# Attention layers: the queries' norm factor moved into the scale of the row extremes, and the keys' second copy made by a transfer

## The chip, the cores and the metric

The kernel runs on one core of a Trainium2 chip. The metric is device time in microseconds. The kernel before was timed three times: 1247.73, 1248.68 and 1249.45 us, median 1248.68.

## The reference

A decoder trunk of four pre-norm residual layers over 256 tokens of width 1024, all in float32. Each layer adds a token mixer and then a SwiGLU feed-forward part. The mixers are, in order: native sparse attention (layer 0), block attention (layer 1), a short gated convolution (layer 2), and native sparse attention again (layer 3). What matters here is that every part begins with a norm, and that the attention scores are a softmax over scaled products of queries and keys:

```
def rms_norm(x, g):
    y = xf * lax.rsqrt(jnp.mean(xf * xf, axis=-1, keepdims=True) + RMS_EPS)
    return (y * g.astype(jnp.float32)).astype(x.dtype)
...
a = rms_norm(h, norm_mix[i])
q, k_c, v_c, k_s, v_s, k_w, v_w, gates = jnp.split(a @ w_in, NSA_SPLITS, axis=-1)
q = q.reshape(B_, S_, G, R, dh) * (HEAD_DIM ** -0.5)
s_win = jnp.einsum('bnqgrd,bnkgd->bgrnqk', qb, kwb)
p_win = masked_softmax(s_win, wmask)
```

The sparse attention has 16 query heads in 4 key groups of 64 elements. It adds three results per head with gates: attention over compressed keys (15 blocks made by a small two-layer network), over selected blocks, and over a window. With 256 tokens the last two see the same causal mask and differ in their keys and values. The block attention is a causal attention with 16 heads here.

## The kernel before, in words

The activations are kept transposed (channels on the 128 partitions, 256 tokens along the free dimension), in eight pieces. The norm is split. Its gain is multiplied in before the projections (`prep`). Its per-token factor, `rstd`, is only known later, so it is multiplied into each projection's result: `rms_tokens` (L239) makes `rstd` with tokens on partitions, `rms_rows` (L246) spreads it as `rb`, the same 256 factors on every partition, and `scaled` (L409) multiplies a projection's result in PSUM with `rb` into an SBUF row. That multiplication is L411.

Precision is kept by splitting each float32 operand into a rounded high part and a remainder, the low part. A weight part of 8 tiles of 128x128 is loaded (`load_part`, L98), its high part copied by ScalarE (L119) and its low part subtracted by VectorE or GpSimd (L123). A product then takes three matmuls (`mm3`, L143 to L145): high with high, high weight with low activation, low weight with high activation. `take` (L126) hands out weight tiles in stream order; it also runs the jobs that are queued in `self.jobs` once the stream has come to the part that they name.

In the sparse attention (`nsa`, L549) the order of steps is written out by hand in `NSA_ORDER`: K is a projection of keys, q one of queries (two heads each, eight in all), F, E, C and D the compression network, c the attention over compressed keys, V the values, s the scores of two heads with their softmax, t and T transposes, P the product with the values. The Tile framework then schedules: it keeps to this order as a priority but puts on each engine's queue what it reckons ready first. The queues, SyncE's DMA queue among them, run strictly in that planned order.

The scores in the sparse attention are taken with one matmul of full depth for the high parts: a query tile holds the high part of one head on 64 partitions and its low part on the other 64 (`project_q`, L612 to L620). For that the keys must stand on both halves of the partitions. `put_keys` (L581 to L590) scales a key projection, and for each of its two groups writes the high part to its own half (L587) and to the other half (L588) with ScalarE, and the low part to both halves with two VectorE subtractions (L590). There are four key projections in each sparse layer, so 8 groups.

`scores` (L761) fills three PSUM banks with tag A, of which there are four; a projection takes one of the same four. `softmax` (L432) then works on each head in four pieces: for each piece one VectorE instruction adds the mask, multiplies by -0.125 and takes the row minimum (L441), ScalarE takes the exponential with its sum (L444), VectorE the reciprocal (L446), and GpSimd multiplies by the reciprocal and the gate (L448). That makes 64 L441 instructions in a sparse layer and 32 in the block layer, where `moba` (L474) has its own `project_q` (L494) that splits a scaled query. `compressed` (L702) adds a mask to the compressed scores with tokens on partitions (L717).

Of the kernel before, what the change touches and what calls it, by code (L numbers as in the profile page):

```python
# [9 lines left out]
F32 = mybir.dt.float32  # L10
F32R = mybir.dt.float32r
AF = mybir.ActivationFunctionType
OP = mybir.AluOpType
# [3 lines left out]
P = 128  # L17
D = 1024
S = 256
KT = D // P  # L20
NT = S // P
# [4 lines left out]
QSCALE = 0.125  # L26
NEG = -3.0e38
PART = 8
# [20 lines left out]
LAG = 4  # L49
PROJ_BANKS = "AABB"  # L50
PR = ["gpsimd"]
KEY_LO = ["vector", "vector"]
OWN = "vava"
CONE = "vector"
NPAIR = 8
# [4 lines left out]
class Kernel:  # L60
# [178 lines left out]
    def rms_tokens(self):  # L239
        nc = self.nc  # L240
        v = self.sb([P, NT], "var")
        nc.vector.tensor_scalar(v, self.sums[:, :NT], 1.0 / D, EPS, op0=OP.mult, op1=OP.add)
        self.rstd = self.sb([P, NT], "rstd")
        nc.gpsimd.tensor_tensor(out=self.rstd, in0=v, in1=self.mhalf, op=OP.pow)

    def rms_rows(self):  # L246
        nc = self.nc
        pb = self.bank("B")
        for t in range(NT):
            nc.tensor.transpose(pb[:, t * P:(t + 1) * P], self.rstd[:, t:t + 1].to_broadcast([P, P]), self.ident)  # L250
        self.rb = self.sb([P, S], "rb", bufs=1)
        nc.vector.tensor_copy(self.rb, pb[:, :S])
# [179 lines left out]
    def softmax(self, cols, gates):  # L432

        nc = self.nc
        pr = self.sb([P, 3 * S], "pr", bufs=PR_BUFS)
        mn = self.sb([P, 4], "mn", bufs=3)
        den = self.sb([P, 4], "den", bufs=3)
        rc = self.sb([P, 4], "rc", bufs=3)
        for j, (src, c) in enumerate(cols):
            n = c.stop - c.start  # L440
            nc.vector.tensor_tensor_reduce(pr[:, c], src, self.mask[:, S - n:], -QSCALE, 3.0e38, OP.add, OP.min,  # L441
                                           mn[:, j:j + 1])
        for j, (src, c) in enumerate(cols):
            nc.scalar.activation(pr[:, c], pr[:, c], AF.Exp, bias=mn[:, j:j + 1],  # L444
                                 scale=-1.0, accum_out=den[:, j:j + 1])
        nc.vector.reciprocal(rc, den)  # L446
        for j, (src, c) in enumerate(cols):
            getattr(nc, PR[j % len(PR)]).tensor_scalar(pr[:, c], pr[:, c], rc[:, j:j + 1], gates[j], op0=OP.mult, op1=OP.mult)  # L448
        return pr
# [24 lines left out]
    def moba(self, norm):  # L474
        nc, at = self.nc, self.begin(norm)
# [17 lines left out]

        def project_q(p):  # L494
            q = self.ff([P, 2, S])
            self.project([lambda x: self.split(q, self.scaled(x))], at)
            qs.append(q)

        def scores(p):
# [28 lines left out]
        def weigh(p):  # L528
# [8 lines left out]
            for i in range(2):  # L537
# [4 lines left out]
            outs.append(d)  # L542

        self.steps(MOBA_ORDER, {"V": lambda _: self.values(at, put_values), "k": project_k, "q": project_q,
                                "s": scores, "T": turn, "P": weigh})
        self.out_proj(outs, norm + 1)


    def nsa(self, j, norm):  # L549
        nc, at = self.nc, self.begin(norm)  # L550
# [9 lines left out]
        for a in range(2):  # L560
            nc.gpsimd.memset(xs[a][:, 512:], 0.0)
            x = xs[a][:, 512:640].rearrange("p (r c) -> p r c", c=16)
# [15 lines left out]
            self.project([put_raw(a, gp) for a in range(2) for gp in range(2)], at)  # L578


        def put_keys(b, gp):  # L581
            def put(p):
                f = self.scaled(p)
                for i in range(2):
                    kk = self.keys[2 * gp + i]
                    r, o = slice(i * DH, (i + 1) * DH), slice((1 - i) * DH, (2 - i) * DH)
                    nc.scalar.copy(kk[r, 0, b, :], f[r])  # L587
                    nc.scalar.copy(kk[o, 0, b, :], f[r])  # L588
                    for eng, d in zip((getattr(nc, e) for e in KEY_LO), (r, o)):
                        eng.tensor_tensor(out=kk[d, 1, b, :], in0=f[r], in1=kk[r, 0, b, :].bitcast(F32),  # L590
                                          op=OP.subtract)
            return put

        gates = self.sb([P, NT, 48], "gates", bufs=1)
# [17 lines left out]
        def project_q(_):  # L612
            q = self.ff([P, 2, S])

            def put(p):
                f = self.scaled(p)
                for i in range(2):
                    r, o = slice(i * DH, (i + 1) * DH), slice((1 - i) * DH, (2 - i) * DH)
                    nc.scalar.copy(q[r, i, :], f[r])
                    nc.vector.tensor_tensor(out=q[o, i, :], in0=f[r], in1=q[r, i, :].bitcast(F32), op=OP.subtract)  # L620

            self.project([put], at)
            qs.append(q)
# [3 lines left out]
        pc = []  # L627
# [74 lines left out]
        def compressed(gp):  # L702

            p = self.bank(CMP_BANK)
            for i in range(8):
                q = qs[4 * gp + i // 2][:, i % 2, :]
                for n, c in enumerate((112, 240)):
                    mm(p[:, :S], zk[:, 2 * gp + i // 4, c - 16 * i:c - 16 * i + P], q, start=(i == 0 and n == 0),
                       stop=(i == 7 and n == 1))
            sc = self.row()  # L710
            nc.scalar.copy(sc, p[:, :S])
            pq = self.bank(CMP_BANK)
            for t in range(NT):
                nc.tensor.transpose(pq[:, t * P:(t + 1) * P], sc[:, t * P:(t + 1) * P], self.ident)
            pc = self.row()
            p3 = pc.rearrange("p (h c) -> p h c", c=16)
            nc.vector.tensor_tensor(out=pc, in0=pq[:, :S], in1=self.cneg, op=OP.add)  # L717
            mx = self.sb([P, 16], "cmx")
            bc = mx[:, :, None].to_broadcast([P, 16, 16])
            nc.vector.tensor_reduce(out=mx, in_=p3, op=OP.max, axis=AX.X)  # L720
            nc.vector.tensor_tensor(out=p3, in0=p3, in1=bc, op=OP.subtract)
            nc.scalar.activation(pc, pc, AF.Exp, scale=QSCALE)
            getattr(nc, CONE).tensor_tensor(out=pc, in0=pc, in1=self.cone, op=OP.mult)
            nc.vector.tensor_reduce(out=mx, in_=p3, op=OP.add, axis=AX.X)
            nc.vector.tensor_scalar(mx, mx, 1e-30, None, op0=OP.max)
            nc.vector.reciprocal(mx, mx)
            m2 = mx.rearrange("p (t h) -> p t h", t=NT)
            nc.vector.tensor_tensor(out=m2, in0=m2, in1=gates[:, :, 8 * gp:8 * gp + 8], op=OP.mult)
            nc.vector.tensor_tensor(out=p3, in0=p3, in1=bc, op=OP.mult)
            ph = self.sb([P, 16, 2, 16], "ph", F32R, bufs=1)  # L730
            nc.scalar.copy(ph[:, :, 0, :], p3)
            nc.vector.tensor_tensor(out=ph[:, :, 1, :], in0=p3, in1=ph[:, :, 0, :].bitcast(F32), op=OP.subtract)
            phs.append(ph)
# [88 lines left out]
        def project_keys(i):  # L822
            self.project([put_keys(i // 2, i % 2)], at)
# [220 lines left out]
```

## Time and profile before

| | |
|---|---|
| timed runs | 1247.73, 1248.68, 1249.45 us |
| span of the profiled execution | 1247.6 us |
| busy: TensorE, VectorE, ScalarE, GpSimd | 1225.3, 875.0, 675.6, 227.3 us |
| weight loads | 384 of 512 KB, 4.3 us each to landing |
| mean DMA rate | 182 GB/s |

No separate time is given for the profiled execution beside its span; the median of the timed runs is 1.1 us above that span. In the groups of instructions a row names the line, the engine and operation, what it writes and reads, the shape and the count; then the busy time in us and the mean duration in ns, and after the last bar the idle time of the engine just before and what ended it. In a timeline row the first number is the start in us from the span's start, the second the duration. A matmul's duration there includes the depth of the pipeline: matmuls start every 0.12 us for 256 columns and every 0.23 us for 512, though one is listed with 0.28 or 0.39. So a busy TensorE may still be standing, and its stalls are read from the waits and the starts. `PEclk` is the granted TensorE clock, 1.00 at full speed.

### The profile page before, as it was taken

How to read it: one execution, taken by the hardware profiler on the slowest of the kernel's cores; microseconds unless marked ns; L12 is line 12 of the kernel's file. 1: busy time of each engine (PE TensorE's matmuls, PEld its weight loads, DVE VectorE, ACT ScalarE, POOL GpSimd, SP SyncE). 2: the span in 40 equal slices, each digit the busy share in tenths (PEclk: the TensorE clock that was granted, in tenths of full speed). 3: DMA queues.
4: the chain of work that ended last, by engine and by line, in shares of the span. 5: the costliest groups of instructions: out<-in, count | busy, mean ns of one | idle time of the engine just before them, and what ended most of it. 6: DMA issues, size and time to landing. Idle time of an engine off the chain costs nothing.

```text
span 1247.6 us, 19344 instructions
## 1 busy us (share of the span) xinstructions
PE 1225.3 (98%) x6788; PEld 1061.5 (85%) x6788; DVE 875.0 (70%) x1653; ACT 675.6 (54%) x1218; POOL 227.3 (18%) x357
## 2 busy tenths in 40 slices
PE   8999999999999999999999999999999999999997
PEld 8987888888899888888888888888899878888886
DVE  7778785665778795656769886565747797756553
ACT  5588754544456544545444545454446896555443
POOL 1067600000111520000113210000220676000000
PEclk9998999999999999999999999999999999999999
DMA  8741166767555347666665666776666312676772
GB/s 288 247 126 49 52 220 198 239 198 231 188 170 153 102 140 209 216 212 208 220 196 167 195 201 195 212 236 195 208 204 210 118 38 71 208 228 213 226 224 72
DMA packets 91585, 227.20 MB, mean 182 GB/s; under 512 B 17504, under 2 KB 38368, under 8 KB 91488
## 3 DMA queue, kind: packets, MB, share of 16 engines
q1 hardware_dynamic: 91056, 225.41, 57.6%
q8 instruction: 53, 0.87, 0.3%
q10 hardware_dynamic: 432, 0.56, 0.1%
q14 instruction: 44, 0.36, 0.1%
HBM read 213.33 MB, written 1.05 MB: 172 GB/s over the span
## 4 chain that ended last, share of the span: by engine, by line
PE 87%; DVE 5%; ACT 4%; POOL 2%; issue 1%; DMA 1%; POOLq 0%; ACTq 0%; DVEq 0%
PE psA L163 13%; PE psA L167 7%; PE psB L347 6%; PE psB L349 6%; PE psB L348 6%; PE psA L348 5%; PE psA L349 5%; PE psA L347 5%; PE psA L143 2%; PE psB L640 2%; PE psA L144 2%; PE psA L145 2%; PE psB L163 2%; DVE wlo L123 2%; PE psC L349 2%; PE psC L347 2%
## 5 line engine op out<-in xcount | busy, mean ns | idle before, releaser
L123 DVE TENSOR_TENSOR wlo<-raw,whi 128x1024 fp32r<-128x1024 f32 (+1 forms) x366 | 441.0, 1215 | 261.7 <-ACT whi L119 213.7
L119 ACT CAST whi<-raw 128x1024 fp32r<-128x1024 f32 (+1 forms) x379 | 393.2, 1039 | 425.9 <-PE psC L349 91.3
L163 PE MATMUL psA<-ff,whi 128*128 128x512 f32 x686 | 181.5, 393 | 0.1
L163 PEld LDWEIGHTS psA<-ff,whi 128*128 128x128 f32 x686 | 124.6, 189 | 22.7 <-DVE row L847 0.6
L347 PE MATMUL psB<-whi,at 128*128 128x512 f32 x352 | 137.6, 391 | 0.2 <-ACT pr L304 0.2
L349 PE MATMUL psB<-whi,at 128*128 128x512 f32 x352 | 137.2, 390 | 0.0
L348 PE MATMUL psB<-wlo,at 128*128 128x512 f32 x352 | 137.1, 389 | 0.0
L230 POOL TENSOR_TENSOR ssq<-ssq,row 128x256 f32<-128x256 f32 x42 | 33.6, 799 | 393.0 <-ACT row L228 392.2
L143 PE MATMUL psA<-at,whi 128*128 128x256 f32 x352 | 101.3, 288 | 2.0 <-DVE row L411 2.0
L167 PE MATMUL psA<-ff,wlo 128*128 128x256 f32 x686 | 101.5, 283 | 0.0
L167 PEld LDWEIGHTS psA<-ff,wlo 128*128 128x128 f32 x686 | 96.2, 191 | 5.3
L145 PE MATMUL psA<-at,wlo 128*128 128x256 f32 x352 | 99.9, 284 | 0.0
L144 PE MATMUL psA<-at,whi 128*128 128x256 f32 x352 | 99.9, 284 | 0.0
L349 PE MATMUL psA<-whi,at 128*128 128x512 f32 x256 | 99.7, 389 | 0.0
L347 PE MATMUL psA<-whi,at 128*128 128x512 f32 x256 | 99.7, 389 | 0.0
L348 PE MATMUL psA<-wlo,at 128*128 128x512 f32 x256 | 99.7, 389 | 0.0
L448 POOL TENSOR_SCALAR pr<-pr,rc,gates 128x256 f32<-128x256 f32 (+1 forms) x128 | 73.7, 590 | 112.6 <-DVE rc L446 111.3
L347 PEld LDWEIGHTS psB<-whi,at 128*128 128x128 f32 x352 | 66.1, 188 | 14.0 <-ACT pr L304 0.6
L349 PEld LDWEIGHTS psB<-whi,at 128*128 128x128 f32 x352 | 66.1, 188 | 13.8
L348 PEld LDWEIGHTS psB<-wlo,at 128*128 128x128 f32 x352 | 66.1, 188 | 13.6
L123 POOL TENSOR_TENSOR wlo<-raw,whi 128x256 fp32r<-128x256 f32 x96 | 69.6, 763 | 36.7 <-ACT whi L119 16.6
L444 ACT ACTIVATE pr<-pr,mn 128x128 f32<-128x128 f32 (+1 forms) x160 | 71.2, 448 | 5.7 <-DVE mn L441 5.0
(239 smaller groups left out, 2256.1 us busy)
## 6 DMA issues: line engine op xcount, KB each, us to landing
raw<-in_w SPq DMA_DIRECT2D x384, 512.0 KB, 4.3
pt<-pt SPq DMA_DIRECT2D x320, 32.0 KB, 3.1
wf<-in_w SPq DMA_DIRECT2D x16, 512.0 KB, 4.5
h<-in_xt SPq DMA_DIRECT2D x4, 256.0 KB, 4.5
raw<-in_w SPq DMA_DIRECT2D x4, 256.0 KB, 4.8
pt<-pt SPq DMA_DIRECT2D x64, 16.0 KB, 2.9
w<-in_w SPq DMA_DIRECT2D x2, 256.0 KB, 3.9
pt<-in_gfin SPq DMA_DIRECT2D x1, 512.0 KB, 3.9
```

Of the source, the lines that this page charges most:

```text
L119: copy(hi[:, c], src[:, c])
L123: eng.tensor_tensor(out=lo[:, d], in0=src[:, d], in1=hi[:, d].bitcast(F32), op=OP.subtract)
L143: mm(out, wt[0], act[0], start=first, stop=False)
L144: mm(out, wt[0], act[1], start=False, stop=False)
L145: mm(out, wt[1], act[0], start=False, stop=last)
L163: mm(outs[o], w[0], acts[k].rearrange("p i s -> p (i s)"), start=(k == 0), stop=(k == n - 1))
L167: mm(outs[o][:, :S], w[1], acts[k][:, 0, :], start=False, stop=False)
L347: mm(o, a[:, 0, s], hi, start=(k == 0), stop=False)
L348: mm(o, a[:, 0, s], lo, start=False, stop=False)
L349: mm(o, a[:, 1, s], hi, start=False, stop=(k == KT - 1))
L444: nc.scalar.activation(pr[:, c], pr[:, c], AF.Exp, bias=mn[:, j:j + 1], scale=-1.0, accum_out=den[:, j:j + 1])
L448: getattr(nc, PR[j % len(PR)]).tensor_scalar(pr[:, c], pr[:, c], rc[:, j:j + 1], gates[j], op0=OP.mult, op1=OP.mult)
```

## The change

It has these parts. The queries are no longer multiplied by the norm factor: `project_q` of both attentions splits the projection straight from PSUM. In its place `rms_tokens` makes a second column, `rneg`, which is `rstd` times -0.125, in the three attention layers' norms, and L441 uses it as its scale instead of the constant (tokens stand on the partitions there, so the factor of a row is one number per partition). In `compressed` the one addition of the mask becomes two of half the width that first multiply by `rstd`. The keys' copy on the other 64 partitions is no longer computed: each group's high and low part, 64 partitions with two runs of 1 KB, are copied by a DMA on SyncE's queue, which is queued as a job for the next weight part. Last, the framework's scratch for DMA descriptors is set to 1024.

```
@@ rms_tokens
+        if self.norm in (0, 2, 6):
+            self.rneg = self.sb([P, NT], "rneg")
+            nc.gpsimd.tensor_scalar(self.rneg, self.rstd, -QSCALE, 1.0, op0=OP.mult, op1=OP.mult)
@@ softmax
-            nc.vector.tensor_tensor_reduce(pr[:, c], src, self.mask[:, S - n:], -QSCALE, 3.0e38, OP.add, OP.min,
-                                           mn[:, j:j + 1])
+            nc.vector.tensor_tensor_reduce(pr[:, c], src, self.mask[:, S - n:], self.rneg[:, j // NT:j // NT + 1],
+                                           3.0e38, OP.add, OP.min, mn[:, j:j + 1])
@@ moba, project_q
-            self.project([lambda x: self.split(q, self.scaled(x))], at)
+            self.project([lambda x: self.split(q, x)], at)
@@ nsa
+        copies = []
+
+        def double():
+            while copies:
+                nc.sync.dma_start(*copies.pop(0))
+
         def put_keys(b, gp):
...
                     nc.scalar.copy(kk[r, 0, b, :], f[r])
-                    nc.scalar.copy(kk[o, 0, b, :], f[r])
-                    for eng, d in zip((getattr(nc, e) for e in KEY_LO), (r, o)):
-                        eng.tensor_tensor(out=kk[d, 1, b, :], in0=f[r], in1=kk[r, 0, b, :].bitcast(F32),
-                                          op=OP.subtract)
+                    nc.vector.tensor_tensor(out=kk[r, 1, b, :], in0=f[r], in1=kk[r, 0, b, :].bitcast(F32),
+                                            op=OP.subtract)
+                    copies.append((kk.bitcast(F32)[o, :, b, :], kk.bitcast(F32)[r, :, b, :]))
+                self.jobs.append((self.pos // PART + 1, double))
@@ nsa, project_q
-            def put(p):
-                f = self.scaled(p)
+            def put(f):
@@ compressed
-            nc.vector.tensor_tensor(out=pc, in0=pq[:, :S], in1=self.cneg, op=OP.add)
+            for t in range(NT):
+                c = slice(t * P, (t + 1) * P)
+                nc.vector.scalar_tensor_tensor(pc[:, c], pq[:, c], self.rstd[:, t:t + 1], self.cneg[:, c], op0=OP.mult,
+                                               op1=OP.add)
@@ kernel
-    nc = bacc.Bacc("TRN2", target_bir_lowering=False, num_devices=1)
+    nc = bacc.Bacc("TRN2", target_bir_lowering=False, num_devices=1, dynamic_dma_scratch_size=1024)
```

More of the change, by code (lines that the diff above doesn't have):

```diff
@@ L51 @@
 PR = ["gpsimd"]
-KEY_LO = ["vector", "vector"]
 OWN = "vava"
```

## The prediction

> **What bounds the kernel now.** I read the page first: span, busy time by engine, chain.
>
> ```profile
> span 1247.6 us, 19344 instructions
> PE 1225.3 (98%) x6788; PEld 1061.5 (85%) x6788; DVE 875.0 (70%) x1653; ACT 675.6 (54%) x1218; POOL 227.3 (18%) x357
> PE 87%; DVE 5%; ACT 4%; POOL 2%; issue 1%; DMA 1%; POOLq 0%; ACTq 0%; DVEq 0%
> ```
>
> TensorE carries 87% of the chain, and the change takes no matmul away. It can only win where TensorE stands, so I listed what TensorE waits for, and then cut the span into windows: the stretch from the end of the compression matmuls to the first scores in both sparse-attention layers (46 to 66, 949 to 969), the tails of both (100 to 123, 1015 to 1026), and the block-attention layer's tail.
>
> ```profile
> PE psB L786 <- POOL pr L448: 2.1, 4, 0.8
> PE psA L143 <- DVE row L411: 2.0, 2, 1.4
> core 0: us, PE busy (x) PEld busy (x) DVE busy (x) ACT busy (x) POOL busy (x), PEclk, DMA share, GB/s
> 46.00:66.00 20.00, 19.37 (x157) 18.66 (x156) 19.56 (x47) 13.92 (x29) 0.00 (x0) 1.00 0.57 187
> 100.00:116.00 16.00, 13.71 (x93) 11.21 (x91) 14.20 (x63) 15.35 (x54) 13.21 (x24) 0.99 0.21 67
> 116.00:123.00 7.00, 6.99 (x25) 5.50 (x26) 4.84 (x15) 3.81 (x13) 5.95 (x11) 0.54 0.00 1
> 949.00:969.00 20.00, 18.59 (x151) 17.88 (x150) 18.32 (x44) 13.73 (x27) 0.00 (x0) 1.00 0.58 180
> 1015.00:1026.00 11.00, 8.98 (x52) 6.44 (x51) 10.44 (x45) 10.31 (x36) 8.53 (x16) 1.00 0.16 48
> 418.00:440.00 22.00, 20.50 (x128) 17.28 (x127) 17.52 (x52) 12.11 (x40) 9.98 (x19) 1.00 0.28 88
> ```
>
> Two kinds of stall come out. In the key stretches VectorE is the full engine (19.56 of 20 us, 18.32 of 20), and the named wait is L411, the multiplication by the norm factor, with 2.0 us in two places. In the tails VectorE, ScalarE and GpSimd are all busy (10.44, 10.31 and 8.53 of 11 us), and TensorE stands for GpSimd's normalising multiply, L448, which the change does not touch. The two places of the L411 wait, from TensorE's timeline, with VectorE's work ahead of the longer one:
>
> ```profile
> 62.59 0.38 PE L143 MATMUL psA<-at,whi 128*128 128x256 f32 x1 [0.63 <-DVE row L411]
> 963.17 0.64 PE L767 MATMUL psA<-keys,ff 128*128 128x256 f32 x4
> 963.64 1.08 PE L770 MATMUL psA<-keys,ff 128*128 128x512 f32 x4
> 966.13 0.38 PE L143 MATMUL psA<-at,whi 128*128 128x256 f32 x1 [1.41 <-DVE row L411]
> ...
> 958.24 1.67 DVE L590 TENSOR_TENSOR keys<-row,keys 64x256 fp32r<-64x256 f32 x4
> 963.91 1.71 DVE L590 TENSOR_TENSOR keys<-row,keys 64x256 fp32r<-64x256 f32 x4
> 965.64 0.43 DVE L411 TENSOR_TENSOR row<-psA,rb 128x256 f32<-128x256 f32 x1
> ```
>
> At 963.17 a query projection is finished and the first scores begin; they take three of the four A banks. The next projection needs the fourth, which the query projection still holds: VectorE is busy with the keys (963.91) and reads that bank only at 965.64.
>
> **The change part by part.** The rows for the prices, by line and shape, and the shortest transfer inside SBUF:
>
> ```profile
> L590 DVE TENSOR_TENSOR keys<-row,keys 64x256 fp32r<-64x256 f32 x32 | 13.3, 417 | 1.1 <-ACT keys L587 0.5
> L588 ACT CAST keys<-row 64x256 fp32r<-64x256 f32 x16 | 6.5, 404 | 0.4
> L411 DVE TENSOR_TENSOR row<-psA,rb 128x256 f32<-128x256 f32 x46 | 19.0, 420 | 3.5 <-PE psA L145 2.9
> L441 DVE CUSTOM_DVE_ANT_0 pr<-psA,mask 128x256 f32<-128x256 f32 x80 | 31.7, 416 | 0.3 <-PE psA L508 0.2
> L859 DVE TENSOR_SCALAR row<-gu,cw 128x256 f32<-128x256 f32 x8 | 2.8, 354 | 0.3
> L652 DVE TENSOR_SCALAR row<-row 128x256 f32<-128x256 f32 x2 | 0.6, 288 | 0.0
> L620 DVE TENSOR_TENSOR ff<-row,ff 64x256 fp32r<-64x256 f32 x32 | 13.7, 427 | 1.8 <-ACT ff L619 0.9
> L541 DVE TENSOR_TENSOR ff<-psC,ff 64x256 fp32r<-64x256 f32 x16 | 6.7, 418 | 3.6 <-ACT ff L540 3.2
> L540 ACT CAST ff<-psC 64x256 fp32r<-64x256 f32 x16 | 5.9, 367 | 10.1 <-PE psC L145 7.5 <-DVE ff L541 2.5
> L244 POOL TENSOR_TENSOR rstd<-var,mhalf 128x2 f32<-128x2 f32 x8 | 6.6, 822 | 106.3 <-DVE var L242 106.3
> pt<-pt SPq DMA_DIRECT2D x320, 32.0 KB, 3.1
> ```
>
> *Keys.* Half of the 32 subtractions L590 and all 16 copies L588 go: per sparse layer 8 x 0.417 = 3.3 us of VectorE and 8 x 0.404 = 3.2 us of ScalarE. All of it lies before the values' projection; two of the four key projections (2 x 2 x 0.417 = 1.7 us of VectorE) lie between 958 and 966.
>
> *Queries.* 24 multiplications L411 go (8 in each sparse layer, 8 in the block layer): 0.42 us each, 0.34 where nothing depends on the one before (below). What read the SBUF row now reads PSUM: by L541 beside L620 a subtraction costs the same (418 and 427 ns), by L540 beside L588 a copy 0.04 us less. [...]
>
> *Row extremes.* 160 L441 instructions take their scale from a column instead of a constant. No row shows that form. The nearest are one operation with a column and with a constant: L859 354 ns, L652 288, so 66 ns more. Nor is that only latency:
>
> ```profile
> 667.51 0.48 DVE L860 SCALAR_TENSOR_TENSOR row<-gu,cw,row 128x256 f32<-128x256 f32 x1
> 667.91 0.42 DVE L847 TENSOR_TENSOR row<-psA,row 128x256 f32<-128x256 f32 x1
> 668.25 0.48 DVE L861 SCALAR_TENSOR_TENSOR row<-gu,cw,row 128x256 f32<-128x256 f32 x1
> ```
>
> L860, with a column, holds VectorE for 0.40 us before L847 starts; L847, without one, for 0.34. Bounds: 0 (the unit loads the column under the instruction before) and 66 ns. I take 60, the difference of these starts: 160 x 0.06 = 9.6 us of VectorE, 3.8 per sparse layer. That is more than the L411 of a sparse layer give back (8 x 0.42 = 3.4). A gain is excluded, since nothing leaves L441.
>
> *Compressed scores.* One addition per call becomes two of half the width with a column, each between 0.20 (half of L860's 0.40) and 0.40; at 0.27, nearer the half, +0.2 us against one of 0.34, in four calls. *rneg:* one tiny GpSimd instruction in three layers, between 0 and 0.8 us (L244), tens of us before its first reader: nothing. The smaller descriptor scratch moves only addresses: nothing. What hides both is that no engine waits on them; rneg uncovered would cost its 0.8 us.
>
> *The copy.* 16 transfers of 128 KB inside SBUF, on SyncE's queue, each waiting for a copy and a subtraction. The nearest rows are 32 KB, 3.1 us to landing, and the 512 KB weight loads at 4.3, so 3.1 to 4.3. Behind the waiting transfer stand the weight loads, and behind those the splits. The loads are issued right after a split frees a buffer, on the same VectorE queue that makes the keys, so the transfer waits for at most one key put, under 2 us, for loads that run buffers ahead: nothing on the path, up to 1 us per layer if a split stands. The readers are the first scores. In the second sparse layer the third key projection's subtractions end at 959.91 now, about 0.8 us earlier after; plus 0.4 issue and 3.1 to 4.3 makes 962.6 to 963.8. The scores start at 963.17. Covered at the low end, 0.6 us late at the high one; I take the low one, since 128 KB is nearer to 32 than to 512.
>
> *The sum.* In the key stretches the query bank now comes free after two copies and two subtractions instead of one multiplication and a long queue: about 1.5 us after the projection (2 x 0.37 + 0.42 behind the last copy, and starts), so near 964.6, when the scores end, against 966.1. Both waits go but for some 0.05 us: 0.63 + 1.41 = -2.0 us. That needs VectorE to be free, and it is: 1.7 us of keys are gone ahead of it. What is late next is the values' projection, 11 us of dense matmuls, which hides the 16 extremes of the first two scores. In the tails stand six scores of 8 extremes per layer: 48 x 0.06 = 2.9 us more VectorE, less three L411 (1.1). On the chain of the first tail I find some ten extremes, of 0.20 to 0.34 each, such as
>
> ```profile
> 125.56 0.34 DVE pr L441
> ```
>
> so at most 10 x 0.06 + 0.2 = 0.8 us per layer, at least 0 (ScalarE's exponentials are behind). I take 0.35 each: +0.7. The block layer's tail (12 extremes, 0.7 us more, less one or two L411, 0.4 to 0.8): even. Total -2.0 + 0.7 = -1.3 us on the profiled span of 1247.6, so 1246.3; the median of the runs is 1.1 us above that span (1248.68; 1247.73 to 1249.45), and I carry the 1.1: **1247.4 us**.
>
> **The rivals.** *The column costs nothing.* Then the tails get lighter by their L411: -2.0 - 0.3 to -0.8, so 1245.9 to 1246.4. For it: L441 is a custom program whose loads the trace does not show. Against: L859 and L860. Chance 0.15.
>
> *The clock of the first tail comes back.* From 116 to 123 the granted clock is 0.54, in the second layer's tail 1.00. Had these 7 us run at full clock they would have taken 7 x 0.54 = 3.8: -3.2, so 1247.4 - 3.2 = 1244.2. For it: both tails have the same work, one is throttled and one isn't, so it hangs on little. Against: the waits for L448 that thin TensorE out before it remain. Chance 0.18; the reverse, a throttled second tail, is in the range's upper end. [...]
>
> *Slower: the query's bank is held too long in the tails.* Before, L411 freed it; after, two copies and two subtractions must have run on engines that are full:
>
> ```profile
> 87.97 0.42 DVE L411 TENSOR_TENSOR row<-psA,rb 128x256 f32<-128x256 f32 x1
> 91.66 0.82 ACT L619 CAST ff<-row 64x256 fp32r<-64x256 f32 x2
> 92.17 0.85 DVE L620 TENSOR_TENSOR ff<-row,ff 64x256 fp32r<-64x256 f32 x2
> ...
> 92.01 0.37 PE L143 MATMUL psA<-at,whi 128*128 128x256 f32 x1
> 94.96 0.64 PE L767 MATMUL psA<-keys,ff 128*128 128x256 f32 x4
> ```
>
> That bank is free at 88.4 now and would be at 93.0. The next query projection starts at 92.0 and can take a bank of the scores before it; the scores that then need three banks start at 95.0: 2 us of slack. From 2 us more delay on, TensorE stands before each of three scores, by about 0.9 us, in both layers: +5.4 - 1.3, so 1252.8. For it: ScalarE is at 15.35 of 16 us there. Against: the slack, and shorter puts. Chance 0.15.
>
> *The copy arrives late* (4.3 us): the scores of the second layer wait 0.6 us, the first layer's about as much: 1248.6. Chance 0.12.
>
> **How the numbers follow.** Forecast 0.40, rivals 0.15, 0.18, 0.15 and 0.12. What a measurement here can tell is about 0.2%, 2.5 us: below 1246.2 is faster, above 1251.2 slower. Faster: the clock 0.18, 0.09 of the free column, 0.12 of the forecast (tails at the low bound, 1246.7, and a little luck of the order): 0.39. Slower: 0.13 of the held bank and 0.04 of the rest: 0.17. Same: 0.44. The range takes in the clock rival and stops short of the held bank: 1243.0 to 1251.6. The forecast's own range is 1246 to 1249.
>
> **What would show it.** In the profile after: 24 fewer L411; L590 at 16, L588 gone; 16 issues of 128 KB. L441 at about 476 ns for 128x256; at 416 the column is free. The wait of L143 at the first scores under 0.3 us in both layers; if a bank's wait moves to ScalarE or to L620's successor in the tails, the held bank was right. The windows 116 to 123 at clock 0.54 or 1.00 decide the second rival. A first score waiting for DMA would be the last one. The forecast is wrong if the key stretch keeps its wait, or if the tails lose more than 1.6 us together.

## The result, and the profile after

The changed kernel took 1260.41 us (median of 4 runs, 1258.55 to 1262.0), the kernel before 1249.07 beside it (4 runs, 1247.73 to 1249.7): ratio 1.0091, 95% interval 1.0076 to 1.0105. It is 11.3 us slower, where 1247.4 was forecast.

The page of the changed kernel, its span, its busy times and its chain:

```profile
span 1259.5 us, 19343 instructions
PE 1226.3 (97%) x6788; PEld 1060.3 (84%) x6788; DVE 871.1 (69%) x1617; ACT 669.0 (53%) x1202; POOL 227.9 (18%) x360
PE 82%; DVE 5%; ACT 4%; POOL 3%; DMA 2%; issue 2%; SPq 2%; POOLq 0%; ACTq 0%; DVEq 0%
```

VectorE and ScalarE have less to do than before (871.1 against 875.0, 669.0 against 675.6), TensorE has the same (1226.3 against 1225.3), and the span is 11.9 us longer: TensorE stands more. Groups of instructions by shape show that each instruction costs what it was priced at: the extremes 471 and 343 ns (416 and 282 before, so 55 and 61 more; 57 in experiment 3), a query's copy 367, a subtraction from PSUM 422 (418 in the block layer, on 128 partitions). The last line is from the list of transfers.

```profile
L443 DVE CUSTOM_DVE_ANT_0 pr<-psA,mask,rneg 128x256 f32<-128x256 f32 x80 | 36.5, 471 | 0.3
L443 DVE CUSTOM_DVE_ANT_0 pr<-psA,mask,rneg 128x128 f32<-128x128 f32 x80 | 25.9, 343 | 0.9 <-PE psA L777 0.4
L627 DVE TENSOR_TENSOR ff<-psA,ff 64x256 fp32r<-64x256 f32 x32 | 13.5, 422 | 2.8 <-ACT ff L626 1.9
L626 ACT CAST ff<-psA 64x256 fp32r<-64x256 f32 x32 | 11.7, 367 | 4.6 <-DVE ff L627 4.1
L202 DVE TENSOR_TENSOR ff<-psA,ff 128x256 fp32r<-128x256 f32 x8 | 3.3, 418 | 0.1
keys<-keys SPq DMA_DIRECT2D x16, 128.0 KB, 2.8
```

The shorter extremes in the kernel before:

```profile
L441 DVE CUSTOM_DVE_ANT_0 pr<-psA,mask 128x128 f32<-128x128 f32 x80 | 20.8, 282 | 0.7 <-PE psA L767 0.6
```

What TensorE waits for has changed. The wait for the multiplication (2.0 us) is gone, as forecast, and these stand in the list of waits of the changed kernel:

```profile
PE psB L796 <- POOL pr L450: 4.0, 4, 1.4
PE psA L426 <- DVE ff L627: 3.4, 2, 1.8
PE psA L777 <- DVE mn L443: 3.2, 2, 1.7
PE psB L688 <- DVE row L684: 1.1, 1, 1.1
```

L796 is a transpose of the exponentials, L777 a score (it waits once in each sparse layer's tail, 1.7 and 1.6 us), L688 a product of the compression's last step. L426 is the values' projection, and it waits for the query's last subtraction, L627. The timeline of the last layer shows why. The query's bank is read by ScalarE, VectorE, ScalarE and VectorE in turn, with each engine's other work between, and is free 3.2 us after the first copy began (978.59 to 981.80):

```profile
978.59 0.37 ACT L626 CAST ff<-psA 64x256 fp32r<-64x256 f32 x1
979.86 0.42 DVE L627 TENSOR_TENSOR ff<-psA,ff 64x256 fp32r<-64x256 f32 x1
980.32 0.37 ACT L626 CAST ff<-psA 64x256 fp32r<-64x256 f32 x1
981.37 0.43 DVE L627 TENSOR_TENSOR ff<-psA,ff 64x256 fp32r<-64x256 f32 x1
981.94 0.47 PE L426 MATMUL psA<-whi,at 128*128 128x512 f32 x1 [1.81 <-DVE ff L627]
```

Windows of the changed kernel, moved along with the delay: the two key stretches, the first tail in two parts, the second tail.

```profile
46.00:68.00 22.00, 20.94 (x171) 20.42 (x171) 20.87 (x43) 13.48 (x27) 0.00 (x0) 1.00 0.83 256
955.00:977.00 22.00, 22.00 (x182) 21.66 (x182) 19.73 (x50) 15.45 (x33) 0.13 (x1) 1.00 0.82 227
102.00:118.00 16.00, 12.95 (x88) 10.38 (x87) 13.55 (x49) 13.75 (x44) 12.24 (x22) 1.00 0.22 67
118.00:125.00 7.00, 3.97 (x20) 2.46 (x20) 4.72 (x24) 4.57 (x18) 5.12 (x10) 1.00 0.00 0
1025.00:1037.00 12.00, 9.26 (x53) 6.74 (x54) 10.76 (x43) 9.70 (x34) 7.84 (x16) 1.00 0.01 1
```

In the last layer's key stretch TensorE no longer stands (22.00 of 22 us, and its list of waits for 955 to 977 is empty). In the first it still does, for 1.06 us at 63.88: that is L688's wait for a VectorE copy, L684, which now stands behind a query's subtraction on VectorE's queue (the timeline in the section on the prediction shows both).

From 118 to 125 the clock is whole now (0.54 from 116 to 123 before), but TensorE is busy for 3.97 of 7 us, and no engine is full. The tail does not lack an engine; it lacks the next thing to do.

From TensorE's timeline, how far the kernel is behind the kernel before at seven points (the time before, and the delay in us; "fold", "transfer" and "column" are experiments 1 to 3 below, "column, old order" is experiment 9):

| point | before | changed | fold | transfer | column | column, old order |
|---|---|---|---|---|---|---|
| compression's first matmuls end, layer 0 | 45.92 | +0.25 | +0.11 | +0.61 | +0.11 | +0.28 |
| values' projection ends, layer 0 | 82.95 | +2.12 | +3.97 | +1.79 | +0.26 | +0.70 |
| output projection ends, layer 0 | 158.98 | +4.53 | +6.64 | -0.33 | +2.21 | +0.35 |
| output projection ends, layer 1 | 456.87 | +5.66 | +7.84 | +0.33 | +3.56 | +0.64 |
| compression's first matmuls end, layer 3 | 948.61 | +6.33 | +7.34 | +0.07 | +3.11 | +0.16 |
| values' projection ends, layer 3 | 986.44 | +8.25 | +8.97 | -1.55 | +3.20 | +0.52 |
| output projection ends, layer 3 | 1059.39 | +11.86 | +14.09 | -1.49 | +6.53 | +0.90 |

Most of the loss, 9.8 of 11.9 us, comes in two places of each sparse layer: ahead of the values, and in the tail. The block layer adds 1.1 us.

### The profile page after: what moved, and what is told of

It reads as the page before. It is cut to its first block, busy times and chain, and to the rows that moved or that the text cites. A ratio compares the mean times of both kernels' runs of the same rounds, so it can differ in the third digit from the quotient of the medians.

```text
span 1259.5 us, 19343 instructions
## 1 busy us (share of the span) xinstructions
PE 1226.3 (97%) x6788; PEld 1060.3 (84%) x6788; DVE 871.1 (69%) x1617; ACT 669.0 (53%) x1202; POOL 227.9 (18%) x360
## 4 chain that ended last, share of the span: by engine, by line
PE 82%; DVE 5%; ACT 4%; POOL 3%; DMA 2%; issue 2%; SPq 2%; POOLq 0%; ACTq 0%; DVEq 0%
PE psA L162 13%; PE psA L166 7%; PE psB L349 6%; PE psB L351 6%; PE psB L350 6%; PE psA L350 4%; PE psA L351 4%; PE psA L349 4%; PE psA L142 3%; PE psA L144 3%; PE psA L143 3%; PE psB L647 2%; PE psB L162 2%; DMA raw<-in_w 2%; ACT whi L118 2%
## 5 line engine op out<-in xcount | busy, mean ns | idle before, releaser
L351 PEld LDWEIGHTS psB<-whi,at 128*128 128x128 f32 x352 | 66.1, 188 | 13.8
```

Source lines behind the costliest of these rows:

```text
L351: mm(o, a[:, 1, s], hi, start=False, stop=(k == KT - 1))
```

## The experiments

Four theories were tried. **Bank (T1):** the query's PSUM bank comes free too late. **Queue (T2):** the transfers hold SyncE's queue and the weight loads behind them. **Column (T3):** the extremes' 55 to 61 ns lie on the path. **Order (T4)** came up after the eighth run: the planner, which puts the instructions on the queues, makes another order of the edited kernel, and the order costs. Times are medians; each run's difference is taken from the kernel before on the same chip (1248.8 to 1249.4).

| # | kernel | us | difference | ratio, 95% interval |
|---|---|---|---|---|
| 1 | fold alone | 1262.68 | +13.6 | 1.0108 (1.0094 to 1.0122) |
| 2 | transfer alone | 1248.07 | -1.1 | 0.9993 (0.9984 to 1.0002) |
| 3 | column alone | 1256.19 | +7.1 | 1.0057 (1.0045 to 1.0070) |
| 4 | change, one hand-over | 1261.12 | +12.0 | 1.0093 (1.0079 to 1.0106) |
| 5 | fold without the column | 1255.20 | +5.8 | 1.0052 (1.0038 to 1.0066) |
| 6 | fold, query copied at once | 1257.96 | +8.5 | 1.0071 (1.0058 to 1.0083) |
| 7 | before, with memsets | 1249.71 | +0.3 | 1.0005 (0.9997 to 1.0014) |
| 8 | transfer alone, later | 1247.09 | -2.4 | 0.9984 (0.9976 to 0.9993) |
| 9 | column alone, old order | 1249.90 | +1.1 | 1.0011 (1.0002 to 1.0020) |
| 10 | before, in the column's order | 1256.55 | +7.7 | 1.0061 (1.0048 to 1.0073) |
| 11 | change, old order | 1270.78 | +22.0 | 1.0176 (1.0162 to 1.0190) |
| 12 | fold alone, old order | 1274.21 | +25.4 | 1.0204 (1.0190 to 1.0218) |
| 13 | transfer alone, later, old order | 1247.55 | -1.3 | 0.9987 (0.9978 to 0.9996) |
| 14 | fold, query copied at once, old order | 1250.57 | +1.7 | 1.0014 (1.0006 to 1.0023) |
| 15 | change without the column, its order | 1258.29 | +9.5 | 1.0077 (1.0064 to 1.0089) |
| 16 | change mended | 1249.29 | +0.5 | 1.0007 (0.9998 to 1.0016) |
| 17 | before, in the change's order | 1269.94 | +20.7 | 1.0170 (1.0156 to 1.0184) |

**1. The fold alone.** From the changed kernel, the second split put back:

```
-   copies.append((kk.bitcast(F32)[o, :, b, :], kk.bitcast(F32)[r, :, b, :]))
-   self.jobs.append((self.pos // PART + 1, double))
+   nc.scalar.copy(kk[o, 0, b, :], f[r])
+   for d in (r, o):
+       nc.vector.tensor_tensor(out=kk[d, 1, b, :], in0=f[r], in1=kk[r, 0, b, :].bitcast(F32), op=OP.subtract)
```

> The fold alone: the queries are read unscaled from PSUM, the extremes take the column, the compressed mask is added in two halves; the keys' copy is made by the second split, as in the kernel before. Three theories share the 11 to 12 us that the change cost. Query's bank (T1): the two halves of the query's put hand the PSUM bank from ScalarE to VectorE and back, so the bank comes free 3 to 4 us after the product instead of 1.5, and the values' projection and the scores behind it are late; most of the loss is then here: 5 to 9 us above the kernel before, with the values' product waiting for the query's subtraction (1.5 and 1.8 us in the changed kernel). SyncE's queue (T2): the transfers of the keys hold the loads behind them; this kernel has none of them and is then within 2 us of the kernel before. Column (T3): 60 ns on each row extreme, chained through the score banks; then the tails grow by 2 to 4 us in each NSA layer here too, and the stretch of the keys not at all.

At least as much as the whole change loses (the two intervals overlap), and more than any of the theories gave. The queue (T2) is not the cause.

**2. The transfer alone.** The changed kernel with `scaled`, the constant scale and the single mask addition put back.

> The transfer alone: the keys' other half is made by 16 transfers of 128 KB, and the queries are scaled, the extremes take the constant and the compressed mask is added at once, as in the kernel before. T2 (SyncE's queue): the loads of weights behind the transfers wait for the keys' subtractions, ScalarE's rounding of the weights waits for the loads, and most of the loss is here: 5 to 8 us above the kernel before, all of it between the end of the compression's weights and the values' projection in the two NSA layers (2 us in the first of them and 2 in the last) and behind it. T1 (the query's bank): 0 to 3 us above. T3 (column): between 2 us below and no change.

No loss; T2 falls. The first layer does lose 1.2 us between the compression and the end of the values (+0.61 to +1.79 in the table), and the last gains 1.6.

**3. The column alone.** The kernel before with the operand's form changed (and the change's smaller descriptor scratch):

```
+   self.rneg = const.tile([P, NT], F32, tag="rneg", name="rneg")
+   nc.vector.memset(self.rneg, -QSCALE)
...
-   nc.vector.tensor_tensor_reduce(pr[:, c], src, self.mask[:, S - n:], -QSCALE, 3.0e38, OP.add, OP.min, mn[:, j:j + 1])
+   nc.vector.tensor_tensor_reduce(pr[:, c], src, self.mask[:, S - n:], self.rneg[:, j // NT:j // NT + 1], 3.0e38, OP.add, OP.min, mn[:, j:j + 1])
```

> The kernel before with one edit: the scale of the row extremes is read from a column in SBUF that holds the constant, so the values are the same and only the operand's form differs. The extremes take 55 to 61 ns more each, 8 us of VectorE's time over the kernel. T3 (the column is on the path): 2 to 5 us above the kernel before, all of it in the stretches of the scores. T1 and T2: 0.5 to 1.5 us above, as the prediction had it for the tails (0.35 us each).

The column takes 7.1 us by itself, all in the tails, as T3 would have it, though T3 gave 2 to 5. It lengthens the extremes by 9.8 us of VectorE's time, and nearly three quarters of that would have to lie on the path. The smaller descriptor scratch is not what costs: experiments 7 (+0.3) and 9 (+1.1) have it too.

**4. One hand-over.** In the changed kernel, both copies ahead of both subtractions:

```
    for i, r, o in halves:
        nc.scalar.copy(q[r, i, :], f[r])
+   for i, r, o in halves:
        nc.vector.tensor_tensor(out=q[o, i, :], in0=f[r], in1=q[r, i, :].bitcast(F32), op=OP.subtract)
```

> The whole change, with both of ScalarE's copies of the query ahead of both subtractions of VectorE, in the NSA layers: the bank is handed over once instead of three times. T1 (the query's bank): ScalarE's second copy no longer waits for the first subtraction (about 1 us for each of the four queries of a layer), and 2 to 5 us of the 11 to 12 come back. T2 (SyncE's queue) and T3 (the column): within 1 us of the changed kernel, since neither the transfers nor the extremes are touched.

ScalarE's idle time ahead of L626 falls from 4.6 to 0.4 us, and nothing comes back. Turn-taking is not the cost; L426 still waits for the last subtraction, 3.0 us instead of 3.4:

```profile
L626 ACT CAST ff<-psA 64x256 fp32r<-64x256 f32 x32 | 11.7, 366 | 0.4
PE psA L426 <- DVE ff L628: 3.0, 2, 1.7
```

**5. The fold without the column.** Experiment 1 with `-QSCALE` in place of `self.rneg`; it leaves out the queries' norm factor.

> The fold without its column: the queries are read unscaled from PSUM and the compressed mask is added in two halves, keys by the second split, but the row extremes take the constant (their norm factor is left out of the computation here). The fold alone measured 13.6 us above the kernel before, the column alone 7.1. If the two are separate costs, this kernel is 5 to 8 us above the kernel before, half of it by the end of the values' projection of the first NSA layer. If the long hold of the query's bank costs only because the extremes are slower too (VectorE as the one full engine), it is within 3 us of the kernel before, since VectorE has 24 multiplications less.

The two parts nearly add up: 7.1 for the column, 5.8 for the rest, 13.6 for both. What each of them is made of is not yet said: all three kernels run in orders of their own (below).

**6. The fold with a prompt copy.** In experiment 1 the query goes to a row first, as the multiplication did:

```
+   def plain(self, p):
+       f = self.row()
+       self.nc.vector.tensor_copy(f, p)
+       return f
```

> The fold with the query's bank freed at once: VectorE copies the unscaled query to a row in SBUF (as long as the multiplication that it replaces), and the split reads the row, as in the kernel before; extremes with the column, compressed mask in two halves. If the held bank is what the fold costs beyond the column, this kernel is where the column alone was: 6 to 9 us above the kernel before and 4 to 8 below the fold alone, and the values' projection waits for no query. If the rest is the compressed scores' two half additions or something else of the fold, it stays at 12 to 15 above.

By the ratios (1.0071 and 1.0108) it is 4.6 us below experiment 1 and near the column alone, and no product waits for the query's subtraction. The late bank, with the order that the planner made around it, is the rest of the fold's cost: the two kernels' matmuls differ in order too, in 212 of 6,788 places of the traces.

**7. Memsets beside the extremes.** The kernel before with `nc.vector.memset(self.spare, 0.0)` behind each extreme (and the smaller scratch).

> The kernel before, with the constant scale, and behind each of the 160 row extremes a VectorE memset of one column that nobody reads (59 ns in the profile of before for this shape). If what the column costs is VectorE's time alone, this kernel loses as much as the column did: 5 to 9 us. If the column costs by something of its own (a wait for its operand, the chain through the extreme's result), it loses at most 2 us, since the extreme's result is there as early as before.

As much more VectorE time as the column adds, in 160 pieces, costs nothing that can be measured:

```profile
L443 DVE MEMSET spare<- 128x1 f32 x160 | 9.4, 59 | 8.9
103.56 0.44 DVE L443 MEMSET spare<- 128x1 f32 x4
```

But the second line (VectorE's timeline) shows four memsets in a row, well behind their extremes: the planner had moved them. So this run bounds VectorE's load and not the delay of an extreme's result. And it pointed to the order. In the traces another matmul than in the kernel before stands in 337 of TensorE's 6,788 places in experiment 3, though it computes the same things; experiment 6 has exactly the sequence of experiment 3. (The expectations of experiments 9, 13 and 14 count instructions in the planned program, 186 and 119 of them; the traces do not record that count.)

**8. The transfer, later.** Experiment 2 with `self.pos // PART + 2`.

> The transfer alone, as in the second run, but queued one weight load later, so that the keys are nearly made when SyncE reaches it. In the run with the transfer alone the first NSA layer lost 1.2 us between the end of the compression and the end of the values' projection, and the loads stood behind waiting transfers. If SyncE's wait is the cause, that loss goes and the time falls 1 to 2 us below the transfer alone, so 2 to 3 us below the kernel before (ratio 0.998). If the landing of the transfer is what the first scores wait for, they wait longer and the time is 0 to 2 us above the transfer alone.

Faster than the kernel before by 2.4 us. The first layer's 1.2 us are gone (the values' projection ends at +0.31), and SyncE's queue stands less before a transfer. Its waits in experiment 2 and here (in all, times, longest):

```profile
SPq L584 <- DVE keys L593: 20.6, 9, 6.4
```

```profile
SPq L584 <- DVE keys L593: 13.8, 7, 3.7
```

**9 and 10. The column in the old order, and the old instructions in the column's order.** The order of one kernel is written into the other as a list of places for TensorE, VectorE, ScalarE and GpSimd. The edges only say which instruction stands first on a queue:

```
+   for a, b in zip(order, order[1:]):
+       tc.add_manual_dep(q[b], q[a].name, mybir.DependencyInfo(
+           mybir.DependencyClass.NoSync, mybir.DependencyReason.DATA), reason="order")
```

> The column alone, as in the third run, with the instructions of TensorE, VectorE, ScalarE and GpSimd held in the order that they have in the kernel before (by edges that order the queues and make no engine wait for another). In the third run the planner had put 186 of TensorE's 6,626 instructions in another place. If the column costs by its 57 ns on each extreme (T3), this kernel is still 5 to 8 us above the kernel before. If it costs by the order that the planner made of it (T4), it is at most 2 us above.

> The kernel before, constant scale and all, with its instructions held in the order that the planner gave to the kernel with the column. If the order is what costs (T4), it loses 5 to 8 us as the column did, with extremes as short as before; if the column's own time is what costs (T3), it stays within 1.5 us of the kernel before.

This decides between T3 and T4 for the column. With 475 ns extremes in the old order the kernel loses 1.1 us; with 413 ns extremes in the new order it loses 7.7. The traces show that the orders are those meant: matmuls run in 9 as in the kernel before, in 10 as in 3, and SyncE's transfers, which no edge holds, stand in one order in all four.

```profile
L452 DVE CUSTOM_DVE_ANT_0 pr<-psA,mask,rneg 128x256 f32<-128x256 f32 x80 | 36.4, 475 | 0.2
```

```profile
L452 DVE CUSTOM_DVE_ANT_0 pr<-psA,mask 128x256 f32<-128x256 f32 x80 | 31.9, 413 | 0.3 <-PE psA L519 0.2
```

(The inserted lines move L441 to L452, and all lines behind by 11.) How an order costs is plainest in the block layer's tail. In the old queue ten products of the output projection stand ahead of a group of transposes, in the new one eight, and the transposes wait for GpSimd that much longer. TensorE's waits there, in the kernel before, in the column alone, and in the kernel before in the column's order:

```profile
432.04 0.33 PE L520 MATMUL psB<-ident,pr 128*128 128x128 f32 x1 [0.23 <-POOL pr L448]
```

```profile
434.27 0.33 PE L520 MATMUL psB<-ident,pr 128*128 128x128 f32 x1 [0.97 <-POOL pr L448]
440.22 0.47 PE L143 MATMUL psC<-pt,ff 128*128 128x512 f32 x1 [0.80 <-DVE ff L541]
```

```profile
436.42 0.33 PE L531 MATMUL psB<-ident,pr 128*128 128x128 f32 x1 [0.91 <-POOL pr L459]
442.37 0.47 PE L154 MATMUL psC<-pt,ff 128*128 128x512 f32 x1 [0.78 <-DVE ff L552]
```

The last two have the same waits, one with the column and one without. Together they make 0.74 + 0.80 = 1.5 us, which is the delay that this layer's output projection adds (+2.00 at the end of its scores, +3.56 behind it in the table).

**11 and 12. The change and the fold in the old order.** The same edges, with the order of the kernel before for all instructions that both have.

> The whole change with TensorE, ScalarE, VectorE and GpSimd held in the order of the kernel before, as far as the instructions are in both; only the changed instructions are new. T4 (the order): most of the 11 to 12 us come back, and the kernel is within 3 us of the kernel before, on either side. T1 (the query's bank, by itself): 4 to 8 us of the loss stay, with TensorE's waits for the query's subtraction. T3: the column's 7 stay.

> The fold alone (keys by the second split) in the order of the kernel before. Free, the fold measured 13.6 us above the kernel before, of which the column alone made 7.1 and the queries' part about 6. T4 (the order): within 3 us of the kernel before. T1 (the bank held by two hand-overs between ScalarE and VectorE): 4 to 8 us above it. If both extremes and bank cost by themselves, 10 to 14.

None of the numbers held: both are far slower than in their own order. TensorE's list of waits in experiment 12 names the query's subtraction, L638 there, six times, 19.1 us together; scores (L788), projections (L153) and the values (L437) wait for it:

```profile
PE psA L788 <- DVE ff L638: 8.7, 2, 4.4
PE psA L153 <- DVE ff L638: 6.1, 2, 3.4
PE psA L437 <- DVE ff L638: 4.3, 2, 2.3
```

In the old order the subtractions stand far down VectorE's queue, since they used to read a row and nobody was in a hurry for them. They now hold a bank until then. So it seems that the planner's new order was partly a cure for the bank, and a column's harmful order came with it; why the planner chose it no run shows.

**13. The later transfer in the old order.**

> The transfer alone, queued one weight load later, with the four engines held in the order of the kernel before. Free, it was 2.35 us faster than the kernel before (ratio 0.9984), but the planner had also moved 119 TensorE instructions. If the gain is the transfer's, VectorE's 16 subtractions and ScalarE's 16 copies less, it stays: 1.5 to 3 us faster, with the two waits for the query's multiplication shorter than 0.63 and 1.41 us. If it was the order's, the kernel is within 1 us of the kernel before.

The gain, 1.3 us (0.5 to 2.7 by the interval), falls just short of the expected 1.5 to 3, but it is the transfer's: the order is held, and both waits for the multiplication are gone from TensorE's list. In the first layer a wait for a transfer stands in their place:

```profile
PE psA L783 <- DMA keys<-keys: 0.9, 1, 0.9
```

**14. The prompt copy in the old order.**

> The fold with the query copied to a row at once by VectorE, in the old order. Free, this kernel was 8.5 us above the kernel before, with the same 186 TensorE instructions moved as for the column. If the fold costs by the late release of the query's bank and by the order, both are gone here, and what stays is the column's own time: 0.5 to 2.5 us above the kernel before. If something else of the fold costs (the halves of the compressed mask, the factor's column), 3 us or more stay.

The fold costs 1.7 us instead of 25.4: with the bank freed at once and the order kept, little more than the column's own 1.1 is left. The two waits for the bank are those of the kernel before, 1.8 us here against 2.0:

```profile
PE psA L153 <- DVE row L429: 1.8, 2, 1.3
```

Put side by side, the four kernels with the fold show that bank and order make nearly the whole of its loss, and that neither cure works alone:

| fold | query read late (split from PSUM) | query copied at once |
|---|---|---|
| planner's own order | +13.6 (1) | +8.5 (6) |
| old order | +25.4 (12) | +1.7 (14) |

The two kernels in the upper row do not share one order, so the table does not divide the 13.6 us between bank and order.

**15. The change without its column, in its own order.**

> The whole change held in its own order, but the row extremes take the constant (the queries' norm factor is left out of the computation here). If the extremes' 57 ns cost by themselves in that order, 2 to 4 us of the 11 to 12 come back; if the order and the bank carry the loss, at most 1.5 us come back.

About 1.8 us come back (ratios 1.0077 and 1.0091, whose intervals overlap), between the two expectations. The extremes' own time is a small part of the loss. The wait for the query stays as it was:

```profile
PE psA L437 <- DVE ff L638: 3.3, 2, 1.8
```

**16. The change mended.** Prompt copy, later transfer, old order.

> The whole change mended: the query is copied to a row at once, the transfer is queued one weight load later, and the engines keep the old order. If the costs found add up (the column's own time about +1, the later transfer about -2), this kernel is 0 to 2 us faster than the kernel before; if the parts hinder each other, it is slower.

The costs found nearly add up: +1.7 and -1.3 make +0.4, measured +0.5 (no difference that can be told), where 0 to 2 us faster was expected. The change can be made harmless. It doesn't pay, because the prompt copy takes as long as the multiplication that the fold removes: in the kernel before a VectorE copy of that shape from PSUM (L252) took 423 ns, the multiplication (L411) 420.

**17. The kernel before in the change's order.**

> The kernel before, with its multiplication of the queries, its constant scale and its second split, held in the order of the changed kernel as far as the instructions are in both. If the changed order is what the change loses by, it loses 7 to 12 us here too. If the changed order is one that suits kernel and queries, and the bank held by two hand-overs costs by itself, the kernel stays within 3 us of the kernel before. Between the two both carry a part: the column's share of the order alone would make about 7.

It loses more than the change itself. An order that suits one set of instructions is bad for the other, in both directions (+22.0 us in experiment 11, +20.7 in 17), so this pair cannot say how much of the change's loss its order makes by itself. The waits that it adds are for GpSimd (L797, a transpose), in the compression's last step (L692) and for the extremes (L435, the values):

```profile
PE psB L797 <- POOL pr L459: 5.5, 5, 2.1
PE psB L692 <- DVE row L688: 5.1, 4, 2.1
PE psA L435 <- DVE mn L452: 4.1, 2, 2.3
```

## Why the prediction was wrong, by its steps

**The step that failed** is in the sum: "On the chain of the first tail I find some ten extremes", "I take 0.35 each". It counted along the chain of the kernel before, as if the changed kernel kept that order; the description of the kernel names the planner, but the prediction has its order only as "a little luck of the order" and gives it no price. In the old order the step's size is right: it allowed +0.7 for the column, experiment 9 shows +1.1 (+0.3 to +2.5). In the order that the planner made of the column, the same instructions cost 7.1, and 7.7 without any column.

**The second step that failed** is a mis-sized term: the bank comes free "about 1.5 us after the projection". For the three queries ahead of each sparse layer's values it was 3.0 to 4.5 us. From the first copy to the last subtraction alone it took 2.4 to 4.3 us, for the last six queries of each sparse layer (1.9 and 2.2 for the first two), because between the two halves stands other work of the same engines: in the last layer's case above ScalarE rounds a weight and VectorE works on the compressed scores and an extreme, and in the first layer VectorE splits a weight, as its timeline in the changed kernel shows:

```profile
63.08 0.42 DVE L627 TENSOR_TENSOR ff<-psA,ff 64x256 fp32r<-64x256 f32 x1
63.53 0.29 DVE L684 COPY row<-row 128x256 f32<-128x256 f32 x1
63.75 1.22 DVE L122 TENSOR_TENSOR wlo<-raw,whi 128x1024 fp32r<-128x1024 f32 x1
65.01 0.43 DVE L627 TENSOR_TENSOR ff<-psA,ff 64x256 fp32r<-64x256 f32 x1
```

And the next in line, the values' projection, was named as the work that hides the rest; it was the one that stood (1.54 and 1.81 us). Its cost together with the planner's order is 4.6 us by experiments 1 and 6, and 5.8 by experiment 5; in the old order 23.7 (experiments 12 and 14).

**What held.** The transfer: nothing on the path, -2.0 us for the two waits. It measured -1.1, -2.4 when queued later, and -1.3 when queued later in the old order, where the two waits are gone. The prices: 60 ns for the column (55 and 61), 0.04 us less for a copy from PSUM (367 against 404), the same for a subtraction (422 from PSUM, 427 from a row; in the block layer 418 against 485 before, so it came out shorter there).

**The rivals.** The clock of the first tail did come back (118 to 125 at 1.00), and brought nothing, since TensorE is starved there. The record bounds its price: beside the experiments the kernel before ran 87 times, 10 times with a mean granted clock of 0.999 or more (median 1248.1 us) and 73 times with 0.997 or less (1249.1), so a whole clock went with about 1 us and not with 3.2. In the kernel before the drop came behind a thin stretch: from 112 to 116 TensorE was busy for 2.15 of 4 us, and its longest single wait there was 0.81 us.

```profile
112.00:114.00 2.00, 0.95 (x4) 0.55 (x4) 1.52 (x10) 1.95 (x8) 1.84 (x4) 1.00 0.66 246
114.00:116.00 2.00, 1.20 (x7) 0.77 (x7) 1.93 (x13) 2.00 (x11) 2.00 (x5) 0.90 0.00 0
```

In the last layer of the changed kernel's profile a drop took its place, behind the wait for the query (1.81 us), where the values' projection took 12.4 us from its first matmul's start to its last one's instead of 10.9:

```profile
980.00:984.00 4.00, 2.19 (x8) 1.71 (x8) 3.91 (x17) 2.91 (x11) 0.74 (x2) 0.89 0.00 0
984.00:988.00 4.00, 4.00 (x14) 3.16 (x13) 2.83 (x10) 2.23 (x8) 3.17 (x4) 0.69 0.14 8
```

The loss does not hang on this drop: the changed kernel's execution with a mean clock of 0.999 took 1259.58 us.

The held bank, priced at +5.4 with a chance of 0.15, is the rival that came true, with its place wrong: TensorE waited ahead of the values, in both layers, and not before three scores of each tail. That its price looks right (4.6 to 5.8, order included) is luck. The late copy was not seen in the changed kernel; in the old order the first scores did wait for a transfer, 0.9 us in experiment 13 and 1.0 in experiment 16. That the planner would reorder the kernel was no rival at all, and by the sum below it carries the larger part.

**What adds up, and what stays open.** Column's order about 7, late bank about 5, transfer about -1 to -2: 10 to 11 of the 11.3 us. This sum uses parts measured one at a time; in the changed kernel the order is a third one (another matmul than with the column alone stands in 269 of 6,788 places), and no run isolates its share there. Why a column makes the planner choose another order was not looked into.

## What to carry to other kernels

Where a planner fills the queues, an edit's price is its instructions plus the order that the planner makes of them: compare the queues' orders of both kernels before reading any difference as an instruction's cost, and hold the order to measure the edit alone. Here the column lost 7.1 us in the planner's order and 1.1 in the old one. A held order can itself be bad for the new instructions (+22.0 and +25.4 us in experiments 11 and 12), so one such run is not enough. An instruction that frees a shared bank was worth its time here though its arithmetic could go elsewhere (+1.7 us with the prompt copy and +25.4 without it, both in the old order): ask who reads the bank last, and what stands ahead of that reader on its queue. The copy moved to a transfer paid here (2.4 us, and 1.3 in the old order) when it was queued later, so that the queue waited less for its source (13.8 us in experiment 8 against 20.6 in experiment 2).

## What the runs showed of the hardware

- One operand's form, a column instead of a constant, took 55 and 61 ns more in the changed kernel, on instructions of 416 and 282 ns, and 57 on both in experiment 3.
- The 16 transfers of 128 KB inside SBUF landed after 2.4 to 6.3 us in the changed kernel, 2.8 in the median.
- The kernel before, its instructions in another order, took 0.6% (experiment 10) to 1.7% (experiment 17) longer.
- In the kernel before a whole clock went with about 1 us of 1249 over 87 executions, though its profile shows a mean of 0.54 from 116 to 123.
